# One chain of product groups over all stages, weight sums in place with a fourth load buffer, and retention statistics in five pieces

## The chip, the cores and the metric

The kernel runs on one core of a Trainium2 chip. The metric is the device time of one execution in microseconds (us), lower is better. Engines are named as in the profile: PE is the matrix engine (TensorE, matmuls), PEld its weight loads, DVE is VectorE, ACT is ScalarE, POOL is GpSimd, and SP is the engine that issues the DMAs. L151 is line 151 of the kernel before.

## The reference

One decoder layer, all in float32, for a batch of 1, 1024 positions and a model width of 2048:

```
mod = silu(c) @ w_ada + b_ada                  -> shift, scale, gate
h   = rms_norm(x, norm_gain) * (1 + scale) + shift
proj = h @ w_in                                -> q k v z (8 heads), and q k v z (8 more heads), 128 each
oa  = stick_breaking_attention(rms_norm(q), rms_norm(k), v) * silu(z)
ob  = head_group_norm(chunkwise_retention(rotary(q), rotary(k), v)) * silu(z)
y   = concat(oa, ob) @ w_out
x   = x + gate * y
```

w_in is 2048 by 8192, w_out 2048 by 2048. The two large products (h times w_in, and the concatenated heads times w_out) make up most of the matrix work. The norm over each retention head needs a mean and a variance over the 128 values of each position and head.

## The kernel before, in words

**The products.** Both large products are cut into groups. A group multiplies 8 of the 16 row blocks of the contraction with 256 columns of the weight, for all 1024 positions. It does so by the scheme of Strassen and Winograd: in place of 8 products of quarters there are 7, named P1 to P7, of sums of quarters. Each float32 operand is split into a high and a low part in a faster format, and each product is hi*hi, lo*hi and hi*lo (`mm3`, L148 to L151) for each of 4 pairs of row blocks (`NP`, L30): 12 matmuls of 128x512. There are 80 groups in five stages. For w_in: e (16 groups, first half of the contraction, columns of the stick-breaking heads, whose sums go to DRAM), f and g (one stage of 32, second half of the contraction: f finishes the columns of e, g begins those of the retention heads) and h (16, first half of the contraction, finishes the columns of g). For w_out: y (8, the stick-breaking heads' half of the contraction) and o (8, the retention heads' half, which finishes y). The letters are those of the tile names: `b_h` is a bank of a group of h.

**The left operands.** They stay in the SBUF as seven combinations (A11, S2, S3, A12, S1, A22, S4), in four parts j each, hi and lo, and each product uses one (`LEFT`, L33). When a stage's last group has used a combination, `tell` (in `run`, L390) asks for the next stage's in its place: `place_later` (L224) queues it, and `tick` (L167) takes one from the queue every two ticks. A placing is `split` (L144): ACT makes the high part (L145), DVE the low part, and for every fourth POOL does (L146). A combination that is needed and not yet placed is placed at once (L374).

**The weights.** `load` (L243) brings half a group's weights (two quarters, 512 KB) into one of three buffers `wr`. `make` (L248) lets POOL form the sums that the scheme needs: T1 = B12 - B11 and T2 = B22 - T1 in tiles of their own, T3 = B22 - B12 in the place of B12, T4 = B21 - T2 in the place of T2 (L255). For each product ACT makes the high part `wh` (`first`, L257 to L261), and DVE the low part `wl` (`second`, L263 to L266), both with three buffers.

**The banks.** P1, P6, P5 and P3 add up in bank b, P7 and P4 in d, P2 is in a. Between them the bank's content is taken out: `ended` (L332) has ACT copy it after P1 (`p`), P6 and P7 (`u`) (L285, with POOL adding the seed, a partial sum of an earlier stage, 6 ticks later, L288), and DVE add after P2, P5, P4 and P3 (L294, L296). P6 must wait for P1's copy, and P3 for P5's addition.

**The order.** `plan` (L306) writes the order of a stage: P1 of a group, then P4 and P3 of the group before, then P6, P7, P2, P5 of the group. It was called once for each of five lists (L544), so that each stage ends P5, P4, P3 of its last group and the next begins P1, P6. It also fixes for each step how many products ahead it is issued. `run` (L356) then issues the products, four ticks each, and at each tick what is due: `at` (L164) sets a step some ticks ahead, `lanes` hold longer tasks as generators that yield a number of ticks. All engines take their instructions in the order of the program; SP issues nearly all DMAs. Attention (`sb_heads`, L961) and retention (`ret_heads`, L1042) run as tasks in between. `drain` (L192) runs ticks until nothing is pending; it stands where SBUF regions change hands: after the first three products of f (L677), and after the last product of y (L1239), before o.

**Two other tasks.** `second_half` (L579) runs during e: it weighs 128 loads of 256 KB of w_ada with silu(c) (L434 on DVE; for the later four of eight parts every second one on ACT and POOL) and from the sums makes the second half of h. It yields 2 ticks for each load. `gather` (L656) waits for its end (`h2`). In retention `values_r` (L1101) has `stats` (L1114) give DVE one row of 20 small instructions: mean and variance of four blocks, and a reciprocal root by a guess and three Newton steps (`rsqrt_newton`, L136). `normal` (L1123) on ACT applies them 6 ticks after the matmuls.

Of the kernel before, what the change touches and what calls it, by code (L numbers as in the profile page):

```python
# [59 lines left out]
def layer_kernel(ctx, tc, x, c, w_ada, b_ada, norm_gain, w_in, sb_q_gain, sb_k_gain, ret_norm_gain, w_out,  # L60
                 rot, ret_mask, ret_kdec, chunk_decay, out):
    nc = tc.nc
# [6 lines left out]
    wp = Ring(ctx.enter_context(tc.tile_pool(name="wp", bufs=1)))  # L69
# [7 lines left out]
    keep = {(n, j): dr.tile([P, HALF], F32, name=f"keep_{n}_{j}") for n in COMBOS for j in range(NP)}  # L77
# [57 lines left out]

    def rsqrt_newton(y, m, u, iters=3):  # L136

        nc.vector.tensor_scalar(y.bitcast(I32), m.bitcast(I32), -0.5, RSQRT_MAGIC, op0=ALU.mult, op1=ALU.add)
# [25 lines left out]
    def at(k, fn):  # L164
        later.append((now[0] + k, fn))
# [67 lines left out]
    class Group:  # L233


        def __init__(self, w, k0, col0, name, **more):
            self.w, self.k0, self.col0, self.name = w, k0, col0, name
            self.seed, self.gate, self.put, self.done, self.pool, self.turns = None, (None, None), None, None, None, False
            self.before = None
            self.__dict__.update(more)  # L240
            self.t, self.parts = {}, {}

        def load(self, i):  # L243
            r = wp.tile([P, NP, 2 * P], F32, tag="wr", bufs=3, name=f"wr_{self.name}_{i}")
            nc.sync.dma_start(r, self.w[:, self.k0 + i:self.k0 + 2 * NP:2, self.col0:self.col0 + 2 * P])
            self.t[f"B{i + 1}1"], self.t[f"B{i + 1}2"] = r[:, :, 0:P], r[:, :, P:2 * P]

        def make(self, n):  # L248

            t = self.t  # L250
            if n in ("T1", "T2"):
                t[n] = wp.tile([P, NP, P], F32, tag=n, bufs=1, name=f"{n}_{self.name}")
            o, a, b = {"T1": ("T1", "B12", "B11"), "T2": ("T2", "B22", "T1"), "T3": ("B12", "B22", "B12"),
                       "T4": ("T2", "B21", "T2")}[n]
            nc.gpsimd.tensor_tensor(t[o], t[a], t[b], op=ALU.subtract)  # L255

# [46 lines left out]
    def on(k, j, fn):  # L303
        events.setdefault((max(k, -9), j), []).append(fn)

    def plan(groups):  # L306
        lo = len(flat)
        for i, g in enumerate(groups):
            g.last = g is groups[-1]
            g.n = len(flat) and flat[-1][0].n + 1  # L310
# [5 lines left out]
        for k in range(lo, len(flat)):  # L316
            g, p = flat[k]
            for q, back, j, fn in (("P1", 5, 0, lambda g=g: g.load(0)), ("P6", 6, 1, lambda g=g: g.load(1)),
                                   ("P6", 4, 1, lambda g=g: g.make("T1")), ("P6", 3, 1, lambda g=g: g.make("T2")),
                                   ("P7", 3, 1, lambda g=g: g.make("T3")), ("P4", 3, 1, lambda g=g: g.make("T4")),  # L320
                                   (p, 2, 0, lambda g=g, p=p: g.first(p)), (p, 2, 2, lambda g=g, p=p: g.second(p))):
                if q == p:
                    on(k - back, j, fn)
        return range(lo, len(flat))

# [29 lines left out]

    def run(ks, tell=lambda n: None, last=None):  # L356

        for k in ks:
            g, p = flat[k]
            if g.turns:  # L360
                turning[0] = now[0] + 30
            if p == "P2" and k + 10 in ks and flat[k + 2][0].last and not g.last:
                tell("")
            if p == "P1":
# [16 lines left out]
            for j in range(NP):  # L381
# [7 lines left out]
                tick()  # L389
            if g.last:  # L390
                tell(LEFT[p])
# [187 lines left out]
    def second_half():  # L579
# [30 lines left out]
        for n, (i, r) in enumerate(order_):  # L610
# [14 lines left out]
            load(n + 3)  # L625
            yield 2
        yield 16
# [44 lines left out]

    run(ks_a, gather)
# [368 lines left out]
    def ret_heads():  # L1042
# [4 lines left out]
        for h in range(NH):  # L1047
# [53 lines left out]
            def values_r(g):  # L1101
# [12 lines left out]
                def stats():  # L1114
                    for j in range(4):
                        nc.vector.bn_stats(st6[:, j, :], op[:, j, :])
                    for j in range(4):
# [115 lines left out]
    def results(g):  # L1233
        return take(lambda n, j: mix[g][j][n], {f"mix{g}_{j}" for j in range(NP)})

    run(ks_b[3:], take(lambda n, j: keep[n, j]))
    run(ks_c, results(0))
    run(ks_y, results(1))
    drain()  # L1239
# [3 lines left out]
    with tc.tile_pool(name="ot", bufs=1, side="right", reuse_waits="tile") as otp:  # L1243
        ot = Ring(otp)
        quarters = {}

        def put_y(i):
            def put(e, hf, t):
                quarters[i, e, hf] = t
            return put  # L1250

        def finish(i):
# [23 lines left out]
        for i, g in enumerate(groups_o):  # L1276
            g.put, g.pool = put_y(i), (ot, 10, 5)
            g.done = lambda i=i: start(finish(i), 2)
        run(ks_o)
        drain()  # L1280
# [52 lines left out]
```

## Time and profile before

| what | us |
|---|---|
| median of the runs (2096.39, 2097.23, 2099.32) | 2097.23 |
| profiled execution | 2098.06 |
| its span, first to last instruction | 2096.0 |
| PE busy | 1961.6 |
| DVE busy | 1417.7 |
| ACT busy | 944.3 |
| POOL busy | 925.1 |

The mean granted clock of PE was 0.974. An engine that is busy for 94% of the span, as PE is, has few gaps; who ended each of them, and where they lie, is what the views in the prediction show. In the table of waits a row names who waited, for whom, the sum, the number of times and the longest. In a timeline a row has start, duration, engine, line, what is written and read, and in square brackets the idle time ahead of it and who ended it. In the table by stretches each engine has its busy time and, in brackets, its instructions; behind them are the granted clock, the share of the DMA engines and what they moved.

### The profile page before, as it was taken

How to read it: one execution, taken by the hardware profiler on the slowest of the kernel's cores; microseconds unless marked ns; L12 is line 12 of the kernel's file. 1: busy time of each engine (PE TensorE's matmuls, PEld its weight loads, DVE VectorE, ACT ScalarE, POOL GpSimd, SP SyncE). 2: the span in 40 equal slices, each digit the busy share in tenths (PEclk: the TensorE clock that was granted, in tenths of full speed). 3: DMA queues.
4: the chain of work that ended last, by engine and by line, in shares of the span. 5: the costliest groups of instructions: out<-in, count | busy, mean ns of one | idle time of the engine just before them, and what ended most of it. 6: DMA issues, size and time to landing. Idle time of an engine off the chain costs nothing. (4 is left out here: it accounts for less than half of the span.)

```text
span 2096.0 us, 27331 instructions
## 1 busy us (share of the span) xinstructions
PE 1961.6 (94%) x9089; PEld 1571.6 (75%) x9089; DVE 1417.7 (68%) x2194; ACT 944.3 (45%) x1718; POOL 925.1 (44%) x627
## 2 busy tenths in 40 slices
PE   5878899998999999999999999899999988997998
PEld 4456677875778777788888888677788867886887
DVE  6778786457657676675555654789787976647565
ACT  4532344444454545554454444445354544435322
POOL 0424587646443334232222312677465754235452
PEclk9889999999999999999999999899999999999999
DMA  8648887423454455443433434768586876356665
GB/s 293 219 150 266 261 265 232 140 87 116 150 184 148 135 152 165 149 149 131 146 121 129 138 111 141 246 211 266 164 276 198 281 262 236 121 179 216 211 191 176
DMA packets 287329, 388.45 MB, mean 185 GB/s; under 512 B 32106, under 2 KB 164276, under 8 KB 287188
## 3 DMA queue, kind: packets, MB, share of 16 engines
q1 hardware_dynamic: 286784, 386.65, 56.9%
q8 instruction: 72, 1.18, 0.2%
q14 instruction: 69, 0.57, 0.1%
q10 hardware_dynamic: 404, 0.05, 0.0%
HBM read 278.51 MB, written 108.10 MB: 184 GB/s over the span
## 5 line engine op out<-in xcount | busy, mean ns | idle before, releaser
L265 DVE TENSOR_TENSOR wl_e_P<-wr_e,wh_e_P 128x512 fp32r<-128x512 f32 x320 | 296.5, 927 | 99.7 <-ACT wh_e_P L260 94.9
L255 POOL TENSOR_TENSOR T_e<-wr_e,T_e 128x512 f32<-128x512 f32 x160 | 236.3, 1477 | 261.8 <-DVE wl_e_P L265 153.2
L265 DVE TENSOR_TENSOR wl_e_P<-T_e,wh_e_P 128x512 fp32r<-128x512 f32 x240 | 237.1, 988 | 149.9 <-ACT wh_e_P L260 149.5
L260 ACT ACTIVATE wh_e_P<-wr_e 128x512 fp32r<-128x512 f32 x320 | 201.2, 629 | 209.3 <-POOL wr_e L255 42.2
L255 POOL TENSOR_TENSOR T_e<-wr_e 128x512 f32<-128x512 f32 x80 | 123.6, 1545 | 229.1 <-DVE wl_e_P L265 209.3
L260 ACT ACTIVATE wh_e_P<-T_e 128x512 fp32r<-128x512 f32 x240 | 150.4, 627 | 114.5 <-POOL T_e L255 50.2
L902 DVE TENSOR_TENSOR_SCAN om<-om 128x128 f32<-128x128 f32 (+2 forms) x96 | 109.1, 1137 | 62.8 <-ACT om L893 61.5
L288 POOL TENSOR_TENSOR u_e<-u_e,c_e 128x512 f32<-128x512 f32 x48 | 69.7, 1453 | 158.0 <-DMA c_e<-part 84.3
L288 POOL TENSOR_TENSOR p_e<-p_e,c_e 128x512 f32<-128x512 f32 x48 | 70.5, 1470 | 143.0 <-DMA c_e<-part 62.7
L255 POOL TENSOR_TENSOR wr_e<-wr_e,wr_e 128x512 f32<-128x512 f32 x80 | 119.2, 1490 | 0.0
L434 DVE SCALAR_TENSOR_TENSOR acc_b<-ada_b,silu_c,acc_b 128x512 f32<-128x512 f32 x88 | 92.0, 1045 | 29.3 <-DMA ada_b<-in_w_ada_dram 28.8
L151 PE MATMUL b_h<-S_h,wl_e_P 128*128 128x512 f32 x192 | 79.7, 415 | 10.8 <-DVE wl_e_P L265 10.8
L151 PE MATMUL b_e<-S_h,wl_e_P 128*128 128x512 f32 x192 | 78.7, 410 | 11.6 <-DVE wl_e_P L265 11.6
L149 PE MATMUL b_e<-S_h,wh_e_P 128*128 128x512 f32 x192 | 77.7, 405 | 8.9 <-ACT p_e L285 5.7
L149 PE MATMUL b_h<-S_h,wh_e_P 128*128 128x512 f32 x192 | 80.3, 418 | 5.6 <-DVE p_e L294 2.9
L150 PE MATMUL b_h<-S_l,wh_e_P 128*128 128x512 f32 x192 | 78.9, 411 | 3.2 <-DVE S_l L146 2.3
L149 PE MATMUL b_g<-S_h,wh_e_P 128*128 128x512 f32 x192 | 76.3, 397 | 2.1 <-ACT S_h L145 2.1
L150 PE MATMUL b_e<-S_l,wh_e_P 128*128 128x512 f32 x192 | 77.3, 402 | 0.0
L149 PE MATMUL b_f<-S_h,wh_e_P 128*128 128x512 f32 x192 | 76.3, 398 | 0.7 <-ACT p_e L285 0.7
L949 PE MATMUL oT<-a,v 128*128 128x256 f32 x320 | 76.9, 379 | 0.0
L151 PE MATMUL b_g<-S_h,wl_e_P 128*128 128x512 f32 x192 | 75.8, 395 | 0.0
L150 PE MATMUL b_g<-S_l,wh_e_P 128*128 128x512 f32 x192 | 75.6, 394 | 0.0
(481 smaller groups left out, 5740.5 us busy)
## 6 DMA issues: line engine op xcount, KB each, us to landing
wr_e<-in_w_in_dram SPq DMA_DIRECT2D x128, 512.0 KB
ada_b<-in_w_ada_dram SPq DMA_DIRECT2D x128, 256.0 KB
c_e<-part SPq DMA_DIRECT2D x128, 256.0 KB
ada_a<-in_w_ada_dram SPq DMA_DIRECT2D x64, 256.0 KB
wr_e<-in_w_out_dram SPq DMA_DIRECT2D x32, 512.0 KB
ld<-fin SPq DMA_DIRECT2D x54, 256.0 KB
part<-p_e SPq DMA_DIRECT2D x48, 256.0 KB
part<-u_e SPq DMA_DIRECT2D x48, 256.0 KB
```

What stands on the lines that cost most here:

```text
L149: nc.tensor.matmul(o, a_hi, b_hi, start=first, stop=False, skip_group_check=True)
L150: nc.tensor.matmul(o, a_hi, b_lo, start=False, stop=False, skip_group_check=True)
L151: nc.tensor.matmul(o, a_lo, b_hi, start=False, stop=last, skip_group_check=True)
L255: nc.gpsimd.tensor_tensor(t[o], t[a], t[b], op=ALU.subtract)
L260: nc.scalar.activation(hi, self.t[RIGHT[p]], AF.Copy)
L265: nc.vector.tensor_tensor(lo, self.t[RIGHT[p]], self.parts[p].bitcast(F32), op=ALU.subtract)
L288: at(6, lambda: nc.gpsimd.tensor_tensor(t, t, o, op=ALU.add))
L434: nc.vector.scalar_tensor_tensor(acc, src, cj, acc, op0=ALU.mult, op1=ALU.add)
L902: nc.vector.tensor_tensor_scan(rev, rev, rev, init, op0=ALU.mult, op1=ALU.bypass)
L949: nc.tensor.matmul(ob, v[:, j, :], a[:, cl], start=diag and ib == 0 and b == 0 and j2 == 0, stop=ch == 0 and ib == 2, skip_group_check=True)
```

## The change

1. `plan` is called once, with all 80 groups. The last group of a stage is now followed by P1 of the next stage's first group, and only then by its own P4 and P3. `until` runs the chain up to a given product; the drains stand after P7 of the first group of f, and after P2 of the first group of o, which takes its buffers from the pool of y.
2. The sums take the places of quarters: T3 in B12, T2 = B11 + T3 in B11 once P1's parts are split off, T1 = B22 - T2 in B12 once P7's are, T4 = B21 - T2 in B21 once P2's are. The tiles T1 and T2 go, and `wr` has four buffers in place of three. The loads are issued 7 and 6 products ahead of P1 (before: 5, and 6 ahead of P6), T3 3 ahead of P1, T2 1 ahead (in the very first group 2), T1 3 ahead of P5, T4 1 ahead of P2 or 4 ahead of P4.
3. Retention's statistics are issued in five pieces, one tick apart, and `normal` 7 ticks after the matmuls in place of 6.
4. `second_half` yields 2 and 3 ticks in turn. Stores of partial sums to DRAM (`to_dram`) are issued 4 ticks after the addition in place of 2.

```diff
-RIGHT = {"P1": "B11", "P6": "T2", "P7": "B12", "P2": "B21", "P5": "T1", "P4": "T2", "P3": "B22"}
+RIGHT = {"P1": "B11", "P6": "B11", "P7": "B12", "P2": "B21", "P5": "B12", "P4": "B21", "P3": "B22"}
...
-    def rsqrt_newton(y, m, u, iters=3):
+    def rsqrt_newton(y, m, u, iters=3, guess=True):
...
-            r = wp.tile([P, NP, 2 * P], F32, tag="wr", bufs=3, name=f"wr_{self.name}_{i}")
+            r = wp.tile([P, NP, 2 * P], F32, tag="wr", bufs=4, name=f"wr_{self.name}_{i}")
...
-            if n in ("T1", "T2"):
-                t[n] = wp.tile([P, NP, P], F32, tag=n, bufs=1, name=f"{n}_{self.name}")
-            o, a, b = {"T1": ("T1", "B12", "B11"), "T2": ("T2", "B22", "T1"), "T3": ("B12", "B22", "B12"),
-                       "T4": ("T2", "B21", "T2")}[n]
-            nc.gpsimd.tensor_tensor(t[o], t[a], t[b], op=ALU.subtract)
+            o, a, op, b = {"T3": ("B12", "B22", ALU.subtract, "B12"), "T2": ("B11", "B12", ALU.add, "B11"),
+                           "T1": ("B12", "B22", ALU.subtract, "B11"), "T4": ("B21", "B21", ALU.subtract, "B11")}[n]
+            nc.gpsimd.tensor_tensor(t[o], t[a], t[b], op=op)
...
-            for q, back, j, fn in (("P1", 5, 0, lambda g=g: g.load(0)), ("P6", 6, 1, lambda g=g: g.load(1)),
-                                   ("P6", 4, 1, lambda g=g: g.make("T1")), ("P6", 3, 1, lambda g=g: g.make("T2")),
-                                   ("P7", 3, 1, lambda g=g: g.make("T3")), ("P4", 3, 1, lambda g=g: g.make("T4")),
-                                   (p, 2, 0, lambda g=g, p=p: g.first(p)), (p, 2, 2, lambda g=g, p=p: g.second(p))):
...
+            if p == "P1":
+                on(k - 7, 0, lambda g=g: g.load(0))
+                on(k - 6, 1, lambda g=g: g.load(1))
+                on(k - 3, 1, lambda g=g: g.make("T3"))
+                alone = g.at["P6"] == k + 1
+                on(k - 2 if alone else k - 1, 3 if alone else 1, lambda g=g: g.make("T2"))
+                on(g.at["P5"] - 3, 0, lambda g=g: g.make("T1"))
+                on(max(g.at["P4"] - 4, g.at["P2"] - 1), 1, lambda g=g: g.make("T4"))
+            on(k - 2, 0, lambda g=g, p=p: g.first(p))
+            on(k - 2, 2, lambda g=g, p=p: g.second(p))
...
-            store(dst[b0 + i][:, hf * HALF:(hf + 1) * HALF], t)
+            store(dst[b0 + i][:, hf * HALF:(hf + 1) * HALF], t, 4)
...
-    ks_a, ks_b, ks_c, ks_y, ks_o = (plan(g) for g in (groups_a, groups_b, groups_c, groups_y, groups_o))
+    plan(groups_a + groups_b + groups_c + groups_y + groups_o)
...
-            yield 2
+            yield 2 + n % 2
...
-    run(ks_b[:3])
+    until(groups_b[0], "P7")
     drain()
...
-                    rsqrt_newton(y, m, u)
-                    nc.vector.scalar_tensor_tensor(m, mv[:, :, 0], -1.0, y, op0=ALU.mult, op1=ALU.mult)
+                    rsqrt_newton(y, m, u, 0)
+
+                def better(last=False):
+                    rsqrt_newton(y, m, u, 1, False)
+                    if last:
+                        nc.vector.scalar_tensor_tensor(m, mv[:, :, 0], -1.0, y, op0=ALU.mult, op1=ALU.mult)
...
-                at(1, stats)
-                at(6, normal)
+                for n, fn in ((1, stats), (2, first_guess), (3, better), (4, better), (5, lambda: better(True)),
+                              (7, normal)):
+                    at(n, fn)
...
-    run(ks_y, results(1))
+    new_left(groups_y, results(1))
+    groups_o[0].put, groups_o[0].pool = put_y(0), groups_y[0].pool
+    until(groups_o[0], "P2")
     drain()
     hd.close()
```

More of the change, by code (lines that the diff above doesn't have):

```diff
@@ L134, in layer_kernel @@
     gate_c = cons.tile([P, KC], F32, name="gate_c")
-    def rsqrt_newton(y, m, u, iters=3):
-        nc.vector.tensor_scalar(y.bitcast(I32), m.bitcast(I32), -0.5, RSQRT_MAGIC, op0=ALU.mult, op1=ALU.add)
+    def rsqrt_newton(y, m, u, iters=3, guess=True):
+        if guess:
+            nc.vector.tensor_scalar(y.bitcast(I32), m.bitcast(I32), -0.5, RSQRT_MAGIC, op0=ALU.mult, op1=ALU.add)
         for _ in range(iters):
@@ L240, in __init__ @@
             self.__dict__.update(more)
-            self.t, self.parts = {}, {}
+            self.t, self.parts, self.at, self.tell, self.early = {}, {}, {}, None, None
         def load(self, i):
-            r = wp.tile([P, NP, 2 * P], F32, tag="wr", bufs=3, name=f"wr_{self.name}_{i}")
+            r = wp.tile([P, NP, 2 * P], F32, tag="wr", bufs=4, name=f"wr_{self.name}_{i}")
             nc.sync.dma_start(r, self.w[:, self.k0 + i:self.k0 + 2 * NP:2, self.col0:self.col0 + 2 * P])
@@ L306, in plan @@
     def plan(groups):
-        lo = len(flat)
         for i, g in enumerate(groups):
-            g.last = g is groups[-1]
-            g.n = len(flat) and flat[-1][0].n + 1
+            g.n = i
             flat.append((g, "P1"))
@@ L315, in plan @@
         flat.extend((groups[-1], p) for p in ("P4", "P3"))
-        for k in range(lo, len(flat)):
-            g, p = flat[k]
-            for q, back, j, fn in (("P1", 5, 0, lambda g=g: g.load(0)), ("P6", 6, 1, lambda g=g: g.load(1)),
-                                   ("P6", 4, 1, lambda g=g: g.make("T1")), ("P6", 3, 1, lambda g=g: g.make("T2")),
-                                   ("P7", 3, 1, lambda g=g: g.make("T3")), ("P4", 3, 1, lambda g=g: g.make("T4")),
-                                   (p, 2, 0, lambda g=g, p=p: g.first(p)), (p, 2, 2, lambda g=g, p=p: g.second(p))):
-                if q == p:
-                    on(k - back, j, fn)
-        return range(lo, len(flat))
+        for k, (g, p) in enumerate(flat):
+            g.at[p] = k
+        for k, (g, p) in enumerate(flat):
+            if p == "P1":
[8 more added lines that the diff above has]
+            on(k - 2, 2, lambda g=g, p=p: g.second(p))
     def prepare(k):
@@ L354, in ended, with run @@
             at(1, add)
-    def run(ks, tell=lambda n: None, last=None):
+    def run(ks):
         for k in ks:
@@ L361, in run @@
                 turning[0] = now[0] + 30
-            if p == "P2" and k + 10 in ks and flat[k + 2][0].last and not g.last:
-                tell("")
+            if p == "P2" and g.early:
+                g.early("")
             if p == "P1":
@@ L389, in run @@
                 tick()
-            if g.last:
-                tell(LEFT[p])
+            if g.tell:
+                g.tell(LEFT[p])
     def store(dst, t, k=2, then=None):
@@ L543, in layer_kernel, with until, new_left @@
     groups_o = [Group(w_out_k, 8, 256 * i, f"o{i}", seed=ypart[2 * i:2 * i + 2]) for i in range(8)]
-    ks_a, ks_b, ks_c, ks_y, ks_o = (plan(g) for g in (groups_a, groups_b, groups_c, groups_y, groups_o))
+    plan(groups_a + groups_b + groups_c + groups_y + groups_o)
+    def until(g, p):
+        done = g.at[p] + 1
+        ks, run_to[0] = range(run_to[0], done), done
+        run(ks)
+    run_to = [0]
+    def new_left(groups, tell):
+        groups[-2].early = groups[-1].tell = tell
     x_norms(0)
@@ L671, in gather @@
             place_later(n, do)
-    run(ks_a, gather)
+    new_left(groups_a, gather)
     for i, g in enumerate(groups_b[:16] + groups_c):
@@ L1116, in stats, with first_guess @@
                         nc.vector.bn_stats(st6[:, j, :], op[:, j, :])
+                def first_guess():
                     for j in range(4):
@@ L1234, in results, with put_y, put @@
         return take(lambda n, j: mix[g][j][n], {f"mix{g}_{j}" for j in range(NP)})
-    run(ks_b[3:], take(lambda n, j: keep[n, j]))
-    run(ks_c, results(0))
-    run(ks_y, results(1))
+    quarters = {}
+    def put_y(i):
+        def put(e, hf, t):
+            quarters[i, e, hf] = t
+        return put
+    new_left(groups_b, take(lambda n, j: keep[n, j]))
+    new_left(groups_c, results(0))
+    new_left(groups_y, results(1))
+    groups_o[0].put, groups_o[0].pool = put_y(0), groups_y[0].pool
+    until(groups_o[0], "P2")
     drain()
@@ L1244, in layer_kernel @@
         ot = Ring(otp)
[L1245 to L1250, printed above, removed]
         def finish(i):
@@ L1276, in layer_kernel @@
         for i, g in enumerate(groups_o):
-            g.put, g.pool = put_y(i), (ot, 10, 5)
+            if i:
+                g.put, g.pool = put_y(i), (ot, 10, 5)
             g.done = lambda i=i: start(finish(i), 2)
-        run(ks_o)
+        until(groups_o[-1], "P3")
         drain()
```

## The prediction

> **What bounds the kernel now.** I read the page first, then the table of waits for TensorE, then busy time by stretches, then each engine in order of time where TensorE stands still.
>
> ```profile
> span 2096.0 us, 27331 instructions
> PE 1961.6 (94%) x9089; PEld 1571.6 (75%) x9089; DVE 1417.7 (68%) x2194; ACT 944.3 (45%) x1718; POOL 925.1 (44%) x627
> ```
>
> PE is without a matmul for 2096.0 - 1961.6 = 134 us. The matmul stream itself (560 products of 12) is left as it is, so a gain comes out of these 134 us and out of the stretches of halved clock behind a wait. Whom PE waits for:
>
> ```profile
> PE b_e L151 <- DVE wl_e_P L265: 15.9, 16, 2.1
> PE b_h L151 <- DVE wl_e_P L265: 10.8, 6, 2.9
> PE b_o L149 <- ACT p_o L285: 10.5, 1, 10.5
> PE b_y L149 <- ACT p_e L285: 8.1, 1, 8.1
> PE b_f L151 <- DVE wl_e_P L265: 6.2, 1, 6.2
> PE d_e L151 <- DVE wl_e_P L265: 5.1, 8, 1.5
> PE b_e L149 <- DVE p_e L294: 3.2, 1, 3.2
> PE b_h L149 <- DVE p_e L294: 2.9, 1, 2.9
> PE b_g L149 <- ACT S_h L145: 2.1, 1, 2.1
> PE b_y L149 <- DVE p_e L296: 2.0, 1, 2.0
> ```
>
> Three kinds. Waits for `wl`, the low half of a weight, in the groups e and h: DVE is late there. Four waits at a stage's end, where P3 needs its bank back from P5's addition (I read the one put to S_h as the same, by its place at the end of g). And waits at a stage's start, where P6 needs the bank back from the copy `p` of P1: 8.1 for y, 10.5 for o, short ones for f and h. How full the engines are there:
>
> ```profile
> core 0: us, PE busy (x) PEld busy (x) DVE busy (x) ACT busy (x) POOL busy (x), PEclk, DMA share, GB/s
> 132.00:230.00 98.00, 88.92 (x393) 70.80 (x391) 84.14 (x110) 27.44 (x47) 41.44 (x25) 1.00 0.82 262
> 460.00:510.00 50.00, 38.44 (x140) 27.14 (x140) 42.85 (x36) 24.36 (x44) 36.22 (x23) 0.90 0.31 100
> 1305.00:1360.00 55.00, 45.71 (x159) 34.09 (x158) 38.83 (x39) 25.27 (x45) 35.50 (x23) 0.84 0.72 245
> 1360.00:1712.00 352.00, 338.19 (x1694) 281.95 (x1694) 292.13 (x503) 165.11 (x295) 220.41 (x144) 0.99 0.72 237
> 1712.00:1742.00 30.00, 19.07 (x70) 15.20 (x69) 22.23 (x61) 13.11 (x27) 6.08 (x5) 0.72 0.66 214
> 1905.00:1930.00 25.00, 12.54 (x48) 9.63 (x47) 18.81 (x22) 13.70 (x23) 11.23 (x8) 0.80 0.78 268
> ```
>
> DVE is at 83 to 86% in the first, second and fourth of these stretches, and at 74 to 75% in the last two, though PE has no matmul for 10.9 and 12.5 us of them. PE is the bound almost everywhere, DVE in patches.
>
> **One chain.** A stage ended P5, P4, P3 and the next began P1, P6. P3 had one product between itself and P5, P6 none between itself and P1. In the chain the next stage's P1 stands ahead of P4, so each of the two spans holds two products. At the end of h:
>
> ```profile
> 1712.90 0.40 PE L151 MATMUL d_h<-A_h,wl_e_P 128*128 128x512 f32 x1
> 1716.17 0.76 PE L149 MATMUL b_h<-S_h,wh_e_P 128*128 128x512 f32 x1 [2.87 <-DVE p_e L294]
> 1722.28 0.39 PE L1108 MATMUL op<-state,r 128*128 128x128 f32 x2
> 1725.93 0.39 PE L150 MATMUL b_y<-A_l,wh_e_P 128*128 128x512 f32 x1
> 1726.16 0.39 PE L151 MATMUL b_y<-A_h,wl_e_P 128*128 128x512 f32 x1
> 1734.61 0.79 PE L149 MATMUL b_y<-S_h,wh_e_P 128*128 128x512 f32 x1 [8.06 <-ACT p_e L285]
> 1739.05 0.53 PE L150 MATMUL b_y<-S_l,wh_e_P 128*128 128x512 f32 x1
> ```
>
> Matmuls start 0.23 us apart (1725.93, 1726.16), so a product is 12 x 0.23 = 2.76 us and covers waits of 3.2, 2.9, 2.1 and 2.0 to within 0.5. P6 gets 5.5 us of cover. After a wait starts are 0.43 apart: 14 rows from 1716.17 to 1722.28 (6.11 us, at full pace 3.22) and 10 from 1734.61 to 1739.05 (4.44 for 2.30) lose 2.9 + 2.1 = 5.0 us more.
>
> The Trainium skill, "TensorE: Matmul & The Clock Gate", section "Why this matters for your kernels", names idle gaps over about 3 us as those that cost the clock. Here 2.87 us did too; by the rule this stage's end would have 2.1 us of clock to give back, not 5.0.
>
> What the removed waits uncover, stage by stage. *e to f* (3.2 us): DVE is busy 42.85 of 50 us, and after that wait P1 of the second f group still waits 6.2 us for `wl` behind the drain's left-operand splits, of which none goes. What PE saves it waits there: 0 (at most 3.2). *g to h* (2.1): at a DMA share of 0.72 the left operands behind it come late too; I take 1. *h to y* (2.9 + 8.1 + 5.0 = 16): with nothing lost 14 of the 30 us would be left, into which DVE's 22.23 us of work do not fit; that alone gives back 8, and what work can slide behind y's start a little more: 10 (5 to 16). *y to o* (2.0 + 10.5): the start wait is ACT working off the drain ahead of P1's copy:
>
> ```profile
> 1911.35 1.14 ACT L145 ACTIVATE A_h<-ld 128x512 fp32r<-128x512 f32 x2
> 1921.20 1.31 ACT L145 ACTIVATE S_h<-ld 128x512 fp32r<-128x512 f32 x2
> ```
>
> These are the first and last of 14 splits after y's P3. In the chain three more products (P6, P7, P2) and P1 come before the drain, 16 ticks, at one split per two ticks 8 splits; 6 remain, behind which P5 and the next P1 still have their weights. 6/14 of 11 us is 4.7, covered by two products (5.5). o0 takes its copies from a pool that needs no attention buffer back. I take 11 of 12.5 (6 to 14 with the clock). Together 0 + 1 + 10 + 11 = 22. New need: A11 two products sooner; its four splits need 8 ticks of 24, nothing.
>
> **The condition's loads.** The 128 loads come every 2.5 ticks, not 2: 1.6 per product, not 2.
>
> ```profile
> L434 DVE SCALAR_TENSOR_TENSOR acc_b<-ada_b,silu_c,acc_b 128x512 f32<-128x512 f32 x88 | 92.0, 1045 | 29.3 <-DMA ada_b<-in_w_ada_dram 28.8
> 132.00:230.00 98.00, 51.89 (x55) 1.00 0.82 262
> 132.00:230.00 98.00, 26.76 (x30) 1.00 0.82 262
> ```
>
> (The two lower rows are L434 and L265 alone, on DVE.) For 30 products DVE works 84.14 us, 2.80 each: over PE's 2.76. The 51.89 us fall by a fifth, 0.35 per product, to 2.45, or 89% of PE's pace; DMA also eases. Of 15.9 + 5.1 = 21 us of waits I take 15; what is uneven stays (5 if DMA, whose landing DVE already awaits for 28.8 us, is the limit; 21 at best). The stretch grows by 64 ticks; h2 comes near tick 397, before tick 404 where gathering asks for it: 7 ticks of cover, beyond which every tick is 0.7 us of PE.
>
> **Retention's statistics.** The burst at the third 2.8 us wait in h:
>
> ```profile
> 1674.00 0.88 DVE L1116 BATCH_NORM_STATS2 st<-op 128x6 f32<-128x128 f32 x4
> 1679.64 0.68 DVE L265 TENSOR_TENSOR wl_e_P<-T_e,wh_e_P 128x512 fp32r<-128x512 f32 x1
> ```
>
> 5.6 us on DVE ahead of a `wl`. In five ticks, that `wl` passes after one or two pieces, some 2 us. No instruction goes; `normal` is one tick later (0.7 us), and its bank is next asked for ticks afterwards. Of the 10.8 us in h I take 6, and 2 for the clock behind them: 8 (2 to 13).
>
> **Sums in place.** Four POOL sums a group, as before:
>
> ```profile
> L255 POOL TENSOR_TENSOR T_e<-wr_e,T_e 128x512 f32<-128x512 f32 x160 | 236.3, 1477 | 261.8 <-DVE wl_e_P L265 153.2
> L260 ACT ACTIVATE wh_e_P<-T_e 128x512 fp32r<-128x512 f32 x240 | 150.4, 627 | 114.5 <-POOL T_e L255 50.2
> L255 POOL TENSOR_TENSOR wr_e<-wr_e,wr_e 128x512 f32<-128x512 f32 x80 | 119.2, 1490 | 0.0
> ```
>
> and two `wl`, the first beside a busy POOL, the second beside an idle one:
>
> ```profile
> 485.45 1.79 DVE L265 TENSOR_TENSOR wl_e_P<-T_e,wh_e_P 128x512 fp32r<-128x512 f32 x1
> 498.53 0.68 DVE L265 TENSOR_TENSOR wl_e_P<-T_e,wh_e_P 128x512 fp32r<-128x512 f32 x1
> ```
>
> In-place form 1490 ns, old forms 1477: no change. T2 gains a product of lead over P6's `wh`, T3 four over P7's; ACT's 50.2 us of waits should shrink. New are waits of POOL: T1 for P7's `wl`, T2 for P1's, T4 for P2's. Behind them on POOL stand seed additions, every fourth left split and rotary products; behind a late T1 ACT's `wh` of P5 and the PSUM copies. From the end of P7's `wl` the loop T1 1.49, `wh` 0.63, P5's `wl` 0.68 to 1.79 is 2.8 to 3.9 us in two products, 5.5: at least 1.6 spare. I take 0 (gain 5, loss 12). On SP the loads move two and three products earlier, past stores and seed loads; the fourth buffer is free by then, except that load 1 follows P3's `wl` by 3 ticks. Stores two ticks later: nothing, their buffers turn over in products.
>
> At the kernel's start P6 follows P1 at once and T2 now waits for P1's `wl`:
>
> ```profile
> 97.33 0.68 DVE L265 TENSOR_TENSOR wl_e_P<-wr_e,wh_e_P 128x512 fp32r<-128x512 f32 x1
> 99.14 0.67 DVE L521 TENSOR_TENSOR acc_a<-ada_sums,acc_a 1x512 f32<-1x512 f32 x1
> ```
>
> P6's `wl` would begin 98.0 + 1.49 + 0.63 = 100.1 and hold L521, on which the first stage depends, by some 2 us: loss 2 (0 to 5; two more weight loads share the DMA there).
>
> **Sum.** 22 + 15 + 8 + 0 - 2 = 43 us off the span of 2096.0: 2053.0. The profiled execution took 2098.06 us, 2.1 beyond its span and 0.8 over the median of 2097.23; on the scale of the median 2097.2 - 43 = 2054.
>
> **Rivals.** *DVE keeps the bound* (0.20): the stage ends' and h's waits come back as `wl` waits, because DVE's work is only moved. For it: 83 to 86% busy. Against: PE's long waits are ACT's. h to y 5, y to o 6, e 5, h 2, start -2: 16 us, 2081. *Spacing alone fails* (0.10), DMA being the limit in e: 10 less, 2064. *All goes* (0.09): e 21, h 13, the stage ends 3 + 2 + 16 + 14 = 35, in all 69, 2028. *The POOL loop* (0.06), the slower one: T1 ends late in e and h, where DVE is already late, and each of these 32 groups waits. It decides once POOL's backlog ahead of T1 passes the 1.6 us spare, which two queued sums (3.0 us) do. At 2 us a group, 64 us: 2054 + 64 = 2118. *The port* (0.06): T1, T4 and the next T3 now stand within 1.25 products. If one more `wl` in each of the 32 groups takes the 1.1 us between 0.68 and 1.79, with no slack, 35 us go: 2089. The Trainium skill, "SBUF — State Buffer", section "The single rule", calls the port that VectorE and GpSimd share an exclusive lock; the 1.79 beside 0.68 agrees.
>
> **How the numbers follow.** The forecast has 0.49. The range 2025 to 2085 holds it with its terms' bounds, the spacing rival and the DVE rival; left out are the POOL loop and the port, 0.12. A run tells some 0.2% (4 us) from no change. Faster by more: 0.49 + 0.19 + 0.10 + 0.09 + 0.04 of the port = 0.91; same 0.03; slower 0.06.
>
> **What would show it.** P3 and P6 at h to y and y to o start with under 1 us of wait, and the clock there is near 1. L151 waits in e fall from 21 to about 6 us, in h from 10.8 to about 5. DVE's burst of L1116 to L1121 is cut by `wl`s. The 6.2 us after the f drain stays or grows. I am wrong if ACT's `wh` waits for T1 grow to reach PE, or if waits for `wl` make up for those that go.

## The result and the profile after

The changed kernel takes 2087.12 us (median of 2088.51, 2083.67, 2088.6, 2085.73). Its ratio to before is 0.9948, 95% interval 0.9931 to 0.9965: 10 us (7 to 14) are gained, where 43 were forecast, and the time lies 2 us above the range. The profiled execution took 2088.51 us.

The page after, span and engines:

```profile
span 2086.7 us, 27289 instructions
PE 1961.6 (94%) x9089; PEld 1565.1 (75%) x9089; DVE 1449.8 (69%) x2194; ACT 940.8 (45%) x1718; POOL 919.8 (44%) x627
```

DVE is busy 32 us longer with the same 2194 instructions, though POOL's time is 5 us less. The table of waits for PE (mm3 is now L150 to L152, `wl` L264, `wh` L259, the sums L254):

```profile
PE b_h L152 <- DVE wl_e_P L264: 14.5, 10, 3.0
...
PE b_e L152 <- DVE wl_e_P L264: 9.7, 12, 2.2
...
PE d_o L152 <- DVE wl_e_P L264: 6.0, 1, 6.0
...
PE otp L1156 <- ACT v L755: 5.5, 3, 1.9
PE d_e L152 <- DVE wl_e_P L264: 4.2, 7, 1.3
PE d_y L152 <- DVE wl_e_P L264: 3.9, 2, 3.1
PE b_y L152 <- DVE wl_e_P L264: 3.6, 2, 2.2
PE a_e L152 <- DVE wl_e_P L264: 3.4, 5, 1.6
```

The waits of a stage's end for a copy or an addition (10.5, 8.1, 3.2, 2.9, 2.0 us before) are gone. In their place y and o wait for `wl`. In e 9.7 + 4.2 + 3.4 = 17.3 us are left of 21.8 (15.9 + 5.1, and 0.8 in `a_e`), and h waits longer than before (14.5 for 10.8).

To see where time comes and goes I count the 560 products in order of issue, from 0, take the start of each one's first matmul in the timeline, and subtract. Outside these seven stretches no kernel differs from before by more than 0.5 us behind its first product (which starts at 103.0 to 105.4 us in all of them):

| us, products | e 0-107 | e to f 108-159 | f and g 160-333 | g to h 334-375 | h 376-445 | h to y 446-459 | y to o 500-519 |
|---|---|---|---|---|---|---|---|
| before | 355.2 | 183.8 | 666.7 | 143.9 | 255.7 | 64.2 | 70.8 |
| after | 345.3 | 185.0 | 670.5 | 135.2 | 268.4 | 59.9 | 65.8 |
| chain alone | 353.0 | 183.3 | 668.3 | 142.6 | 252.4 | 62.7 | 64.3 |
| sums alone | 357.6 | 185.4 | 670.9 | 137.3 | 271.1 | 63.9 | 71.4 |
| pieces alone | 356.7 | 183.0 | 666.7 | 144.7 | 255.8 | 60.3 | 71.8 |
| spacing alone | 338.5 | 183.2 | 667.6 | 143.7 | 255.3 | 63.4 | 70.4 |
| after, later sums, one burst | 336.4 | 184.3 | 667.8 | 139.0 | 260.8 | 59.0 | 67.4 |

The first 40 products of h are in the column g to h; where a time of h is given below, it is that of products 376 to 445. Kernels with the same code in e differ there by up to 5 us (352.2 to 356.7 among four), and in h by 3; smaller differences are not read. The traced execution of chain alone is 6 us under the median of its runs and that of sums alone 6 us over, so their rows add up to more than the medians differ. The change gains in e, at g to h, at h to y and at y to o, and loses 12.7 us in h, where 8 had been forecast as a gain.

My theory after this profile was that the pieces lose h: their short instructions wait beside POOL's sums, and ACT waits for the last piece. The rival was that the new sums lose it whatever the statistics do.

### The profile page after: what moved, and what is told of

It is laid out like the page before. It is cut to its first block, busy times and chain, and to the rows that moved or that the text cites. A ratio compares the mean times of both kernels' runs of the same rounds, so it can differ in the third digit from the quotient of the medians.

```text
span 2086.7 us, 27289 instructions
## 1 busy us (share of the span) xinstructions
PE 1961.6 (94%) x9089; PEld 1565.1 (75%) x9089; DVE 1449.8 (69%) x2194; ACT 940.8 (45%) x1718; POOL 919.8 (44%) x627
## 5 line engine op out<-in xcount | busy, mean ns | idle before, releaser
L264 DVE TENSOR_TENSOR wl_e_P<-wr_e,wh_e_P 128x512 fp32r<-128x512 f32 x560 | 528.4, 944 | 211.8 <-ACT wh_e_P L259 206.3
L254 POOL TENSOR_TENSOR wr_e<-wr_e,wr_e 128x512 f32<-128x512 f32 x240 | 352.8, 1485 | 494.7 <-DVE wl_e_P L264 441.0
L259 ACT ACTIVATE wh_e_P<-wr_e 128x512 fp32r<-128x512 f32 x560 | 350.1, 628 | 253.1 <-PE b_o L151 23.5
L254 POOL TENSOR_TENSOR wr_e<-wr_e 128x512 f32<-128x512 f32 x80 | 112.9, 1411 | 134.4 <-DVE wl_e_P L264 120.3
L915 DVE TENSOR_TENSOR_SCAN om<-om 128x128 f32<-128x128 f32 (+2 forms) x96 | 119.4, 1243 | 57.0 <-ACT om L906 55.2
L287 POOL TENSOR_TENSOR u_e<-u_e,c_e 128x512 f32<-128x512 f32 x50 | 78.2, 1567 | 119.8 <-DMA c_e<-part 84.5
L287 POOL TENSOR_TENSOR p_e<-p_e,c_e 128x512 f32<-128x512 f32 x49 | 73.5, 1500 | 112.4 <-DMA c_e<-part 70.4
L435 DVE SCALAR_TENSOR_TENSOR acc_b<-ada_b,silu_c,acc_b 128x512 f32<-128x512 f32 x88 | 97.5, 1108 | 29.5 <-DMA ada_b<-in_w_ada_dram 28.8
L152 PE MATMUL b_h<-S_h,wl_e_P 128*128 128x512 f32 x192 | 77.3, 402 | 11.8 <-DVE wl_e_P L264 11.8
L152 PE MATMUL b_e<-S_h,wl_e_P 128*128 128x512 f32 x192 | 77.3, 403 | 8.1 <-DVE wl_e_P L264 8.1
L150 PE MATMUL b_e<-S_h,wh_e_P 128*128 128x512 f32 x192 | 76.8, 400 | 5.7 <-ACT p_e L284 5.7
L921 DVE TENSOR_TENSOR be<-be,om 128x127 f32<-128x127 f32 (+2 forms) x96 | 75.0, 781 | 7.8
L150 PE MATMUL b_h<-S_h,wh_e_P 128*128 128x512 f32 x192 | 77.9, 406 | 0.0
L150 PE MATMUL b_f<-S_h,wh_e_P 128*128 128x512 f32 x192 | 76.5, 398 | 0.0
L150 PE MATMUL b_g<-S_h,wh_e_P 128*128 128x512 f32 x192 | 75.7, 394 | 0.0
L152 PE MATMUL b_f<-S_h,wl_e_P 128*128 128x512 f32 x192 | 75.1, 391 | 0.4 <-DVE wl_e_P L264 0.4
L151 PE MATMUL b_f<-S_l,wh_e_P 128*128 128x512 f32 x192 | 75.3, 392 | 0.0
L152 PE MATMUL b_g<-S_h,wl_e_P 128*128 128x512 f32 x192 | 75.1, 391 | 0.0
```

What stands on the lines that cost most here:

```text
L150: nc.tensor.matmul(o, a_hi, b_hi, start=first, stop=False, skip_group_check=True)
L151: nc.tensor.matmul(o, a_hi, b_lo, start=False, stop=False, skip_group_check=True)
L152: nc.tensor.matmul(o, a_lo, b_hi, start=False, stop=last, skip_group_check=True)
L254: nc.gpsimd.tensor_tensor(t[o], t[a], t[b], op=op)
L259: nc.scalar.activation(hi, self.t[RIGHT[p]], AF.Copy)
L264: nc.vector.tensor_tensor(lo, self.t[RIGHT[p]], self.parts[p].bitcast(F32), op=ALU.subtract)
```

## The experiments

### The four parts, each alone

The stores after 4 ticks were not run alone.

**Chain alone**: before with one `plan` call, `until` and `new_left`.

> The kernel before with the one chain alone: old sums T1 to T4, three load buffers, the burst of statistics, the condition's loads every 2 ticks, stores after 2 ticks. The recorded prediction: 22 us faster, nearly all at h to y and y to o. Theory now (VectorE, behind PE at a stage's end, gives back as waits for wl what P3 and P6 no longer wait): faster by what the changed kernel shows at its stage ends, 7 + 5 + 5 = 16 us, e to f 0, with waits for wl of 1 to 3 us behind the first products of y and one of about 6 us behind the drain before o. Rival (the chain itself, by shifting which loads and rotary steps meet h's products, loses the 13 us in h): h some 10 us longer than before, the whole within 5 us of before.

Measured: 2090.02 us, ratio 0.9963 (0.9949 to 0.9977), 8 us gained. (The kernel before took 2097 to 2101 us beside these runs; each ratio is to the runs beside it.) In the trace 6.5 us are gained at y to o and 1.5 at h to y; 3.3 in h and 2.2 in e are within what kernels with the same code differ by. At h to y P3 no longer waits for P5's addition, but P5 itself now waits for its `wl` behind the statistics' burst:

```profile
1718.63 0.80 PE L151 MATMUL b_h<-S_h,wl_e_P 128*128 128x512 f32 x1 [6.23 <-DVE wl_e_P L265]
```

The rival falls (h is 3 us shorter); the theory's size at h to y was still too high.

**Sums alone**: `RIGHT`, `make`, four `wr` and the new ticks of loads and sums.

> The kernel before with the sums in place, the fourth load buffer and the new ticks of loads and sums alone. The recorded prediction: 0, and 2 us lost at the start. Theory that the pieces of the statistics lose h: here h is as long as before within 3 us, the whole between 2 us faster and 4 slower. Rival (the new ticks of POOL's sums make ACT's high halves and so wl late in h, whatever the statistics do): h longer by 8 to 13 us, the whole 8 to 15 us slower than before. The price of the shared port, if the sums in place raise it, would show as mean durations of VectorE's groups above before's without any gain elsewhere.

Measured: 2110.09 us, ratio 1.0056 (1.0034 to 1.0078): 12 us lost, in the trace 15.4 in h, 4 in f and g, and 6.6 gained at g to h. My theory that the pieces lose h fell here: h is lost with the statistics in one burst.

**Pieces alone**.

> The kernel before with the statistics in five pieces alone (the result of the statistics is used one tick later). The recorded prediction: 8 us faster, all in h. Theory now (the short instructions of the pieces each wait about 1 us for a POOL sum beside them, so that the last piece ends some 10 us after the first and ACT waits at the normalisation with PE's copies and high halves behind it): h 5 to 13 us longer than before, the whole 5 to 13 us slower, ACT waiting some 5 us for VectorE's m in each of three places. Rival (the sums in place make h late, not the pieces): no slower than before, up to 8 us faster.

Measured: 2098.03 us, ratio 0.9994 (0.9978 to 1.0011), h 255.8: nothing lost or gained. The ACT wait that the theory named is there. ACT in the stretch 1365 to 1712 us, before and with the pieces:

```profile
ACT be L1125 <- DVE m L1121: 10.7, 5, 2.9
```
```profile
ACT be L1132 <- DVE m L1128: 27.6, 8, 4.6
```

P5's `wl` now slips past, and P1's high half stands behind the waiting `normal`: PE's wait passes to the next product (in one place from 7.0 + 3.7 us for P5 and P1 to 3.1 + 8.3).

**Spacing alone**: `yield 2 + n % 2`.

> The kernel before with the condition's loads at every 2.5 ticks on the mean instead of 2, alone. The recorded prediction: 15 us faster, all in e. Theory now: the loads' work on VectorE is spread over 64 more ticks, so that smaller waits last longer: 9 us faster, as far as the changed kernel's e shows it, with the peak of the gain (about 19 us) near the 60th product, given back to the 90th, and waits for wl of 2 us on the mean left in e. Rival (in the changed kernel the gain in e was cut by the new sums beside it): 15 us here.

Measured: 2081.24 us, ratio 0.9924 (0.9904 to 0.9944), 16 us; in the trace 16.7 in e, as the rival has it. PE's waits there fall from 21.8 to 8.7 us:

```profile
PE b_e L151 <- DVE wl_e_P L265: 6.5, 5, 3.1
...
PE d_e L151 <- DVE wl_e_P L265: 1.5, 1, 1.5
...
PE a_e L151 <- DVE wl_e_P L265: 0.7, 2, 0.4
```

The four logs of ratios add to -0.0064, the change has -0.0052: the parts add, within their intervals. **The change without its sums**, to see whether that holds:

> The changed kernel with the sums as they were (T1 to T4 in their own tiles, three load buffers, old ticks); chain, spacing and pieces stay. If the parts add up, as the four single edits do to within 2 us: ratio to before 1 - 0.0076 - 0.0037 - 0.0006 = 0.988, about 2075 us, 12 faster than the changed kernel, and the 12.7 us lost in h do not appear. Rival (the pieces, in the company of the chain and the new spacing, lose h): h as long as in the changed kernel, 2085 to 2090.

Measured: 2077.35 us, ratio 0.9914 (0.9893 to 0.9936), 10 us under the changed kernel. h falls only to 260.7 (two of three places with statistics take 20.5 and 22.4 us), e to 336.1. The sums are the part that costs most. They are not all of it: the 260.7 us are 5 more than before, and the kernel with chain, spacing and old sums, but one burst ("The parts that pay" below), has 255.2.

### What the sums cost, and through what

The 15.4 us in h lie in three places of four products (P2, P5, P1, P4), 28 products apart: 18.5, 17.9 and 18.3 us before, 23.4, 23.5 and 23.3 with the sums alone. Each holds a burst of statistics, and another ends just ahead of it. The 12 instructions on 128x4 values in a burst (L1119 to L1121), each of which needs the result of the one ahead, are called its string. The middle place, before: the timeline of DVE, then of POOL, then PE's wait.

```profile
1574.14 1.31 DVE L1119 TENSOR_SCALAR m<-mv 128x4 f32<-128x4 f32 x1
1575.49 1.22 DVE L138 TENSOR_SCALAR y<-m 128x4 int32<-128x4 int32 x1
1576.74 0.17 DVE L140 TENSOR_TENSOR u<-y 128x4 f32<-128x4 f32 x1
...
1578.50 0.16 DVE L1121 SCALAR_TENSOR_TENSOR m<-mv,y 128x4 f32<-128x4 f32 x1
1578.58 0.69 DVE L265 TENSOR_TENSOR wl_e_P<-T_e,wh_e_P 128x512 fp32r<-128x512 f32 x1
```
```profile
1574.15 1.28 POOL L288 TENSOR_TENSOR p_e<-p_e,c_e 128x512 f32<-128x512 f32 x1
1575.39 1.29 POOL L255 TENSOR_TENSOR T_e<-wr_e,T_e 128x512 f32<-128x512 f32 x1
1580.09 1.52 POOL L288 TENSOR_TENSOR p_e<-p_e,c_e 128x512 f32<-128x512 f32 x1 [3.41 <-DMA c_e<-part]
```
```profile
1579.32 0.80 PE L151 MATMUL b_h<-S_h,wl_e_P 128*128 128x512 f32 x1 [2.60 <-DVE wl_e_P L265]
```

The same place with the sums alone:

```profile
1583.59 1.30 DVE L1123 TENSOR_SCALAR m<-mv 128x4 f32<-128x4 f32 x1
1584.93 1.18 DVE L138 TENSOR_SCALAR y<-m 128x4 int32<-128x4 int32 x1
1586.15 1.18 DVE L140 TENSOR_TENSOR u<-y 128x4 f32<-128x4 f32 x1
1587.36 0.16 DVE L141 SCALAR_TENSOR_TENSOR u<-u,m 128x4 f32<-128x4 f32 x1
...
1588.15 1.14 DVE L142 SCALAR_TENSOR_TENSOR y<-u,y 128x4 f32<-128x4 f32 x1
...
1589.99 0.69 DVE L263 TENSOR_TENSOR wl_e_P<-wr_e,wh_e_P 128x512 fp32r<-128x512 f32 x1
```
```profile
1583.58 2.51 POOL L253 TENSOR_TENSOR wr_e<-wr_e,wr_e 128x512 f32<-128x512 f32 x2
1586.05 1.25 POOL L286 TENSOR_TENSOR p_e<-p_e,c_e 128x512 f32<-128x512 f32 x1
1588.01 1.26 POOL L286 TENSOR_TENSOR p_e<-p_e,c_e 128x512 f32<-128x512 f32 x1 [0.70 <-DMA c_e<-part]
```
```profile
1590.73 0.80 PE L151 MATMUL b_h<-S_h,wl_e_P 128*128 128x512 f32 x1 [5.77 <-DVE wl_e_P L263]
```

Each of these POOL instructions holds up one short DVE instruction, which takes 0.16 us elsewhere in the string, for its own whole length: the ends pair off (POOL to 1584.87 and 1586.09, DVE to 1584.89 and 1586.11). Before, two POOL instructions meet the string, now four, and T1 meets the string just ahead of the place; each costs some 1.1 us. P5's `wl`, next on DVE behind the string, comes 6.40 us after the string's start instead of 4.44 (1589.99 - 1583.59, 1578.58 - 1574.14). With the 1.1 us of the string ahead that is 3.1 us, and PE waits 5.77 us, not 2.60. The place is 5.6 us longer: 3.2 are this wait, 0.9 lie in P2 (0.6 of them a wait for its `wl`), and 1.5 lie behind the wait, where 11 matmuls start 0.43 us apart and not 5. The Trainium skill, "SBUF — State Buffer", section "Who interferes with whom", says that the engine which takes the shared pair of ports first holds it for its whole instruction and the other blocks fully; these rows agree.

The other possible cause is that the sums come late because they wait for a `wl`. Then ACT's `wh` would wait for them. ACT in the stretch 1365 to 1712 us before, and 1365 to 1730 with the sums alone (in each all rows of `wh` that wait for a sum):

```profile
ACT wh_e_P L260 <- POOL wr_e L255: 20.2, 8, 2.8
ACT wh_e_P L260 <- POOL T_e L255: 12.8, 11, 3.1
```
```profile
ACT wh_e_P L258 <- POOL wr_e L253: 0.7, 2, 0.4
```

33.0 us have become 0.7, so late sums are not what costs h.

Counted over the string of each place and the one ahead of it, the short instructions of over 0.5 us are 2, 2, 2 before and 5, 5, 5 with the sums alone. Three runs move POOL's sums by a product.

In the kernel before T4 a product earlier; in the changed kernel, and with the sums alone, T3 and T4 later:

```diff
-... ("P4", 3, 1, lambda g=g: g.make("T4")),
+... ("P4", 4, 1, lambda g=g: g.make("T4")),
```
```diff
-on(k - 3, 1, lambda g=g: g.make("T3"))
+on(k - 2, 1, lambda g=g: g.make("T3"))
...
-on(max(g.at["P4"] - 4, g.at["P2"] - 1), 1, lambda g=g: g.make("T4"))
+on(g.at["P4"] - 3, 3, lambda g=g: g.make("T4"))
```

> The kernel before with one thing changed: the old sum T4 a product earlier, in the tick of the statistics. Theory: one more POOL sum beside the string in three places of h, each 1.1 us on VectorE; with the clock behind the wait 4 to 6 us longer in h, all of it in the products of P5 and P1 beside the statistics, 2100 to 2103 on the scale of 2097. Rival: 0.

> The changed kernel with its sums in place, but T3 and T4 issued a product later (T3 two products ahead of P1, T4 at three ahead of P4, last tick), so that the pair no longer stands in the tick of the statistics. Theory (two more POOL sums beside the string of 0.16 us instructions, each making one of them last 1.2 us, hold the wl of P5 behind it): h gets back 8 to 13 us, the whole 2074 to 2080. Rival (the in-place sums wait for wl of P7, P1 and P2, and this chain, not the place beside the statistics, is late): h as long as in the changed kernel or longer, since the sums come later still, 2086 to 2095.

> The sums in place alone, with the burst in one piece, T3 and T4 a product later. Theory (the pair of sums in the burst's tick): fewer than 5 of the short instructions last over 0.5 us in each of the three places, the places fall from 23.4 us to 19 to 21, and the whole is 6 to 12 us under the sums in place alone. Rival: 5 stretched ones and 23 us a place as before, the whole at 2108 to 2116.

The theory missed in all three, and the times are those of the rivals: 2099.86 us (ratio 1.0009, 0.9999 to 1.002), 2087.35 (0.995, 0.9933 to 0.9967) and 2113.21 (1.0069, 1.0054 to 1.0084). The counts did not change either: 2, 2, 2 for the first, 5, 6, 6 (after: 6, 6, 6) and 4, 5, 5. DVE is behind: in the middle place the string starts 3.8 us (before) and 5.9 us (sums alone) after the last matmul of `op` starts, and its tick is one tick of 0.7 us after that, so it runs one to two products late. A sum that is moved by a product runs in another order with its neighbours, and as many POOL instructions meet the string. So the tick is not the place, and these runs tested neither the theory nor the rival. The next pair takes the string away instead, by `rsqrt_newton(y, m, u, 0)`:

> The kernel before, with the three Newton steps of retention's statistics left out (9 of the 12 short VectorE instructions of each burst; the normalisation then uses the first guess of the root). It is the base for the next run. Both theories: the waits of 2.6 to 2.9 us beside the statistics in h go, the three places of four products each fall from 18.3 us to about 15, the whole 8 to 14 us under before.

> The sums in place alone, and the Newton steps left out in the same way. Theory (the sums cost h through the string of short instructions that they now stand beside: 5 stretched ones in each place instead of 2): with the string gone the three places take as long as without the sums in place, within 1 us each, and h is within 3 us of the run without Newton steps and sums in place; the whole within 5 us of it. Rival (the sums in place come late by waiting for wl, whatever stands on VectorE): the three places stay 4 to 5 us longer each, the whole 10 to 15 us over it.

Measured: 2080.75 us (0.9913, 0.9896 to 0.9929; 18 us, more than either theory expected, the places at 13.7 each) and 2090.71 (0.9962, 0.9944 to 0.9979). h is 240.6 and 246.0: what the sums cost in h falls from 15.4 to 5.4 us. Two thirds went with the string. In the second kernel 4, 4 and 4 of the six short instructions that the two strings of a place have left are still held up (2, 2 and 1 in the first), two or three more at some 1.1 us each, which is the size of the 5.4 us that stay; that they are their cause was not tested. The other half of the 10 us between the two kernels lies outside h, and its cause is open.

Then the sums alone again, far enough from the string (T3 and T2 behind it, T4 at its tick of before):

```diff
-on(k - 3, 1, lambda g=g: g.make("T3"))
+on(k - 2 if g.at["P6"] == k + 1 else k - 1, 1, lambda g=g: g.make("T3"))
...
-on(k - 2 if alone else k - 1, 3 if alone else 1, lambda g=g: g.make("T2"))
+on(k - 2 if alone else k, 3 if alone else 1, lambda g=g: g.make("T2"))
...
-on(max(g.at["P4"] - 4, g.at["P2"] - 1), 1, lambda g=g: g.make("T4"))
+on(g.at["P4"] - 3, 1, lambda g=g: g.make("T4"))
```

> The sums in place alone, with T3 and T2 two and one products later (one product ahead of P1, and with P1) and T4 at three products ahead of P4, as in the kernel before. Theory (what costs is the number of POOL instructions that run beside the string of short VectorE instructions): 2 or 3 stretched ones in each of the three places instead of 5, the places back from 23.4 us to 18 to 20, and the whole 8 to 14 us under the sums in place alone, 2097 to 2103. Rival (in-place sums are late as such; each waits for a wl): the places stay at 23 us or grow, the whole at 2110 or over.

Measured: 2096.35 us, ratio 0.9989 (0.9974 to 1.0004): 14 us under the sums alone. 3, 3 and 5 short instructions are held up, and the places take 21.0, 20.5 and 21.5 us, more than the 18 to 20 expected. The second string of the middle one:

```profile
1567.73 1.32 DVE L1123 TENSOR_SCALAR m<-mv 128x4 f32<-128x4 f32 x1
1569.08 1.18 DVE L138 TENSOR_SCALAR y<-m 128x4 int32<-128x4 int32 x1
1570.30 0.16 DVE L140 TENSOR_TENSOR u<-y 128x4 f32<-128x4 f32 x1
```
```profile
1567.72 1.29 POOL L286 TENSOR_TENSOR p_e<-p_e,c_e 128x512 f32<-128x512 f32 x1
1568.97 1.27 POOL L253 TENSOR_TENSOR wr_e<-wr_e,wr_e 128x512 f32<-128x512 f32 x1
1572.31 1.66 POOL L286 TENSOR_TENSOR p_e<-p_e,c_e 128x512 f32<-128x512 f32 x1 [2.08 <-DMA c_e<-part]
```

Two POOL instructions meet the string, two short instructions are long. f and g are back at 667.0, and e is 7 us shorter than with the sums alone. In all, the sums in place cost nothing at these ticks: what they cost depends on where they run. In h 6.8 of the 15.4 us are left, which the 7.2 us gained at g to h make up for. The count alone does not give the time of a place: the third has 5 as with the sums alone and takes 21.5 us, not 23.3.

**The changed kernel with these ticks, and with these ticks and one burst:**

> The changed kernel with the sums in place at the same later ticks. Theory: the three places of h, 23.5, 20.8 and 22.3 us in the changed kernel, fall to about 18 to 20 each, and the whole to 2075 to 2081. Rival: the pieces are spread over five ticks, so that POOL's sums meet some of them wherever they are: no change, 2084 to 2090.

> The changed kernel with the sums at the later ticks and the statistics as one burst again. Theory (spread over five ticks, the short instructions meet POOL's in-place sums wherever these stand, and ScalarE waits for the last piece): the three places, 21.1, 23.4 and 23.4 us with pieces, fall to 18 to 21 each, h to 256 to 262 us, the whole to 2068 to 2075. Rival (h is lost to chain or spacing together with the sums in place): h stays at 266 or over, 2077 to 2083.

Measured: 2080.06 us (0.9909, 0.9894 to 0.9923) and 2070.81 (0.9859, 0.9838 to 0.9879). The first time lies in the theory's range by luck: with the pieces h stays at 268.5, its places at 21.1, 23.3 and 23.4 us, and the gain comes from e (336.8) and from f and g (667.8 for 670.5); with one burst h is 260.8. So beside the sums in place the pieces do lose h, 7.7 us. Beside the old sums, with chain and spacing, they lose 5.5 (260.7 in the change without its sums, 255.2 in the parts that pay below). So it is not the sums in place alone that make them cost: my first theory holds in company, not alone.

### The pieces, with a later normalisation

`(7, normal)` becomes `(9, normal)`.

> The statistics in five pieces alone, and the normalisation at the ninth tick instead of the seventh. Theory (with the pieces PE's wait only passes from P5 to P1, since ScalarE stands still 2.8 to 4.6 us for VectorE's m with P1's high half behind it): ScalarE's wait is gone, the three places fall from 18.7 to about 15 us, the whole 6 to 12 us under before. Rival (VectorE has the same work in the same stretch, so that some wl is late in any order): 18 us a place, the whole within 4 us of before.

Measured: 2094.71 us, ratio 0.9981 (0.9967 to 0.9995): 4 us, less than expected. ACT in the stretch 1365 to 1712 us:

```profile
ACT be L1132 <- DVE m L1128: 9.0, 6, 3.8
```

27.6 us have become 9.0. Two places fall to 16.0 and 15.2 us; the middle one does not (19.9): there 4 short instructions are held up, not 2.

### The stage ends

**Later drain**: `until(groups_o[1], "P1")` in place of `until(groups_o[0], "P2")`. In this kernel the second o group takes all its copies from the pool of y, over buffers in which quarters of the first still stand, so part of the output is not the reference's; the instructions are the same ones.

> The changed kernel with the drain between y and o two products later (after P1 of the second o group instead of P2 of the first). Theory (the 6.0 us wait of o0's P4 is the drain's last splits standing ahead of its weights on VectorE and ScalarE): the wait falls below 2 us and 4 to 7 us are gained there, 2080 to 2083. Rival (VectorE has too much work there wherever the drain is): the wait comes back as waits for wl at the next products, the whole within 2 us of the changed kernel.

Measured: 2083.68 us (0.9936, 0.9921 to 0.995); y to o falls from 65.8 to 60.9 us. PE's wait for o0's P4, in the changed kernel and with the later drain:

```profile
1928.18 0.80 PE L152 MATMUL d_o<-A_h,wl_e_P 128*128 128x512 f32 x1 [6.03 <-DVE wl_e_P L264]
```
```profile
1924.13 0.50 PE L152 MATMUL d_o<-A_h,wl_e_P 128*128 128x512 f32 x1 [2.07 <-DVE wl_e_P L264]
```

What stood ahead of that `wl` on DVE in the changed kernel:

```profile
1921.36 1.13 DVE L147 TENSOR_TENSOR A_l<-ld,A_h 128x512 fp32r<-128x512 f32 x1
1922.41 5.11 DVE L147 TENSOR_TENSOR S_l<-ld,S_h 128x512 fp32r<-128x512 f32 x3
1927.44 0.68 DVE L264 TENSOR_TENSOR wl_e_P<-wr_e,wh_e_P 128x512 fp32r<-128x512 f32 x1
```

**The parts that pay**: chain, spacing, stores after 4 ticks, old sums, one burst, later drain (of the second o group P1's copy alone comes from the pool of y).

> The parts that pay, together: one chain, the condition's loads every 2.5 ticks, stores after 4 ticks; the sums and the burst as before; and the drain between y and o moved behind P1 of the second o group, whose P1 copy comes from the pool of the groups before. If the parts add: 2097 - 16 (spacing) - 8 (chain) - 5 (drain) = 2068. If the pieces were worth something beside the chain, it loses a few us against that: 2068 to 2073. Rival (spacing and chain share a gain): 2078 to 2082.

Measured: 2070.2 us, ratio 0.9865 (0.9849 to 0.9882), as the parts add. **And two of four of y's low halves on POOL**, `on_pool=(1, 3)` where the change has `j == 3`:

> The parts that pay, together, and for y's left operands two of each four low halves on POOL instead of one (7 splits off VectorE at h to y). Theory (VectorE's work bounds the end of h): the 14 products around it fall from 61.8 us to 57 to 60, the whole 2066 to 2069. Rival (a split takes 1.3 to 1.8 us on POOL and blocks VectorE's meanwhile, so nothing is won): 61 us or over, 2070 or over.

Measured: 2066.25 us, ratio 0.9846 (0.9829 to 0.9862). h to y is 60.5 us for 61.8, between the two; most of the difference lies in e, where nothing was changed. Not told apart.

**And the pieces with the later normalisation:**

> Chain, spacing, later drain, two of four splits of y on POOL, old sums, and the statistics in five pieces with the normalisation at the ninth tick. If the pieces with the later normalisation bring beside these what they brought alone (4.7 us of h in the trace, 4 us in the median): 2066 - 4 = 2062. Rival (they meet more POOL work in this company, as with the seventh tick and the old sums, where two of the three places took 20 to 22 us): 2066 to 2072.

Measured: 2063.94 us, ratio 0.9821 (0.9807 to 0.9836), the fastest kernel here, 23 us under the changed one. h is 253.0 for 255.8. Whether the last two parts each pay is within the intervals.

## Why the prediction was wrong, step by step

Of the signs that the prediction names, P3 and P6 at the stage ends wait no longer, and one by which it is wrong came: PE's waits for `wl` grow from 39 to 58 us, where 29 us of waits of P3 and P6 go. Of the 33 us that are missing, 14 are missing at the stage ends, 12 at the sums and 7 at the pieces, by the runs of the parts alone; the spacing gave 1 more.

- **Sums in place, 0, is the step whose mechanism failed: 12 us lost.** It priced POOL's time (1490 for 1477 ns) and the loop through T1 and left out what else stood on DVE beside POOL at the new ticks. The rival *The port* had the right resource and the wrong victim: `wl` in h takes as long as before (mean of the 112 there 1.059 and 1.060 us); the string of short instructions is what lengthens. *The POOL loop*, PE behind sums that wait for `wl`, did not come. By POOL's table of waits its sums wait for a `wl` 171 times with the sums alone (61 before), but ACT's waits for sums fall, over the whole kernel, from 95.4 us (53.2 + 42.2) to 35.8: this shrinking was forecast, and PE did not gain by it. A gain of the size of the better bound (5) is there too, 6.6 us at g to h; what makes it was not tried.
- **Pieces, 8: nothing alone, and 5 to 8 us of h lost beside the other parts.** That the `wl` "passes after one or two pieces" was right. "`normal` is one tick later, and its bank is next asked for ticks afterwards" looked at the bank and not at ACT's queue: ACT waits for the last piece with P1's high half behind it. With `normal` two ticks later still, 4 us are gained.
- **Stage ends, 22: 8 in the chain alone.** Of y to o's 11, 4.9 to 6.5 came: six splits were left for the drain as forecast, but they and POOL's work beside them kept DVE until 1927.44, past the two products of cover. Of h to y's 10, 1.5 to 4.3 came. PE's idle time in these 14 products falls only from 11.6 us to 11.2 (chain alone) and 9.3 (changed kernel), and some 9 to 10 us of what is left are waits for `wl`: DVE is behind there, as the rival *DVE keeps the bound* has it, and its 5 and 6 us fit the two stretches. That less work on DVE there would bring it back was tried with y's low halves and not told apart. e to f 0 and g to h 1 agree with the traces, which cannot tell so little from nothing.
- **Spacing, 15: right, 16 alone** (13.1 us of it waits that went). In the changed kernel e gives 9.9 only. The early sums cost the rest: with the later ticks it is 18.4 (355.2 - 336.8). Which of them does it, and why f and g lose 4, was not tried.
- **Start, -2:** the first product starts 0.9 us later, and by the sixth nothing is lost.

With the measured sizes of chain, spacing, pieces and sums the sum is 8 + 16 + 1 - 12 = 13, and 10 came. The range failed because the sums' loss lay at the very end of its bounds (gain 5, loss 12), and over half of the chain's gain and all of the pieces' were missing at the same time.

## What to carry to other kernels

An instruction that is only moved on one engine can cost another: list what runs on the partner of a shared port at the new time, and look for strings of short dependent instructions, each of which can be held up for the partner's whole instruction. The tick at which a step is issued is not when it runs: DVE ran its string one to two products behind its tick, and three moves by a product changed nothing. Measure the parts of a change alone; here 16 us were gained and 12 lost under one ratio of 0.995.

## What was not expected of the hardware

A 0.16 us DVE instruction on 128x4 values takes 1.14 to 1.32 us beside a POOL instruction of 1.25 to 1.30 us, whether it has one input (L1123, L138 of the rows of the sums alone) or two (L140, L142). The four BATCH_NORM_AGGREGATE of 128x6 just ahead are not held up: before, they take 0.36 us together beside a POOL instruction of 1.75 us.
